# Second block's layer norms: shift and factors read in PSUM, weight folded in, bias on ScalarE, two buffers for squares, another order of halves

## The chip, the cores and the metric

The kernel runs on one core of a Trainium2 chip. Its time is the device time of one execution in microseconds; the number that counts is the median over runs.

## The reference, cut to what matters

512 tokens with 1024 features go through two blocks. The change is in the second, at three of its layer norms: the one after the first feed-forward (ln1), the one of the convolution branch (conv_ln) and the one after the mixer (ln2).

```python
def layer_norm(x, g, b):
    mu = jnp.mean(xf, axis=-1, keepdims=True)
    var = jnp.mean(jnp.square(xf - mu), axis=-1, keepdims=True)
    y = (xf - mu) * lax.rsqrt(var + LN_EPS) * g + b

x = layer_norm(alpha * x + 0.5 * swiglu_ffn(x, ...), ln1_g, ln1_b)
m = hybrid_mixer(x, ...)        # its conv branch: silu(layer_norm(u, conv_ln_g, conv_ln_b)) @ w_conv_o
x = layer_norm(alpha * x + m, ln2_g, ln2_b)
x = layer_norm(alpha * x + 0.5 * swiglu_ffn(x, ...), ln3_g, ln3_b)
```

## The kernel before

Activations lie features on partitions: x[0] to x[7] are eight tiles of 128 features by 512 tokens. A projection takes weight tiles of 1 MB or 768 KB (raw), which ScalarE casts to a high part (whi) and VectorE or GpSimd subtracts to a low part (wlo); the operand X is kept as two parts too (Xh by a cast on ScalarE, L291, Xl by a subtraction, L294). Each 128 x 128 block is then three matmuls, Xh with whi (L354), Xl with whi (L355), Xh with wlo (L356). A projection to 1024 features runs in four chunks c of two output tiles, over kt blocks k. The order on each engine is made by the program's scheduler from the order of the code and the dependences; the pictures of it stand in the section on the change.

**Ln** is the layer norm. Sums over features are sums over partitions, so TensorE makes them: tok_sum multiplies an accumulator by a column (1 column of output for every 128 tokens, L202), which puts tokens on partitions. To bring a factor back, diag_of (L189) makes a diagonal matrix of it on VectorE, and spread (L196, L197) multiplies by ones and copies the result from PSUM to SBUF on ScalarE. The steps: pre adds two tiles to st_a; shift1 and shift2 make a rough mean of these (self.s); center subtracts it from each x (L254), squares it on ScalarE into st_q (L261), adds that to st_b on GpSimd (VectorE for the last two, L263) and adds x to st_a on VectorE (L264); fin1 makes mean, variance and the reciprocal root (rstd_of, L172 to L181, with a square root on ScalarE at L174) and two diagonals; fin2 spreads both; norm multiplies (L287) and subtracts (L288). rstd_of also serves the root-mean-square norms and the heads.

**halved** runs the projection ahead of ln1 (kt=6, operand A) and of ln2 (kt=8), in two halves of 256 tokens, HV0 and HV1: for half 0 chunks 0, 1, 2, 3, for half 1 chunks 3, 0, 1, 2. After each chunk the residual is added (L1383). Half 0's centers follow its chunks 2 and 3; its fin1, fin2 and norms lie among half 1's chunks. apply(k) is norm, then weight and bias (VectorE L1433 for even k, ScalarE L1431 for odd k), then the split into Xh and Xl (Xl on GpSimd). **begin** starts the next projection: 48 matmuls of half 0, fin1 of half 1, 24 matmuls, fin2, 24 matmuls, apply of half 1 for all k, then half 1's matmuls. The conv branch's norm cl is an Ln over all 512 tokens: its centers lie in ret_out's chunks, fin1 to norm in the gate stage that follows.

Of the kernel before, what the change touches and what calls it, by code (L numbers as in the profile page):

```python
# [10 lines left out]
F32 = mybir.dt.float32  # L11
# [3 lines left out]
AF = mybir.ActivationFunctionType  # L15
# [34 lines left out]
def tile_net(ctx: ExitStack, tc: tile.TileContext, a, out):  # L50
# [16 lines left out]
    def bank(shape=(P, T), dt=F32):  # L67
        return ps.tile(list(shape), dt, tag="ps", name=nm("ps"))
# [98 lines left out]
        c = prm[name] + i  # L167
        return par[:, c:c + 1]

    def rstd_of(ss, n, eps, scale=1.0):  # L170
        v = sm.tile([P, n], F32, tag="rs_v", name=nm("rv"))
        vec.tensor_scalar(v, ss, scale, eps, op0=ALU.mult, op1=ALU.add)  # L172
        s = sm.tile([P, n], F32, tag="rs_s", name=nm("rs"))
        act.activation(s, v, AF.Sqrt)  # L174
# [24 lines left out]
    def tok_sum(acc, w, tr=FULL):  # L199
        st = bank((P, tr[1] - tr[0]))  # L200
        for i in range(*tr):
            pe.matmul(st[:, i - tr[0]:i - tr[0] + 1], acc[:, i * P:(i + 1) * P], w, start=True, stop=True)  # L202
        return st

    def stile(tag):
        return xp.tile([P, T], F32, tag=tag, name=nm(tag))

    class Rms:
# [21 lines left out]

    class Ln:
        def __init__(self):
            self.sum, self.sq, self.s, self.rb = [stile(f"st_{c}") for c in "absr"]
            self.started = set()
            self.dg, self.dg2 = {}, {}

        def cols(self, tr):
            return slice(tr[0] * P, tr[1] * P)
# [5 lines left out]
        def shift1(self, tr=FULL):  # L244
            st = tok_sum(self.sum, inv_q, tr)
            self.dg[tr] = diag_of(st, tr)

        def shift2(self, tr=FULL):
            spread(self.dg[tr], self.s, tr)

        def center(self, m, tr=FULL, last=False):
            c = self.cols(tr)
            xm = x[m][:, c]
            vec.tensor_tensor(xm, xm, self.s[:, c], op=ALU.subtract)  # L254
            if tr not in self.started:
                self.started.add(tr)
                act.activation(self.sq[:, c], xm, AF.Square)
                act.copy(self.sum[:, c], xm)
            else:
                q = stile("st_q")  # L260
                act.activation(q[:, c], xm, AF.Square)  # L261
                eng = vec if last else pool
                eng.tensor_tensor(self.sq[:, c], self.sq[:, c], q[:, c], op=ALU.add)  # L263
                vec.tensor_tensor(self.sum[:, c], self.sum[:, c], xm, op=ALU.add)  # L264

        def fin1(self, tr=FULL):
            n = tr[1] - tr[0]
            sd = tok_sum(self.sum, inv_d, tr)
            sv = tok_sum(self.sq, inv_d, tr)
            d = sm.tile([P, n], F32, tag="ln_d", name=nm("lnd"))  # L270
            vec.tensor_copy(d, sd)
            v = sm.tile([P, n], F32, tag="ln_v", name=nm("lnv"))
            vec.tensor_tensor(v, d, d, op=ALU.mult)
            vec.tensor_tensor(v, sv, v, op=ALU.subtract)
            r = rstd_of(v, n, LN_EPS)
            self.dg[tr] = diag_of(r, tr)
            vec.tensor_tensor(d, d, r, op=ALU.mult)
            self.dg2[tr] = diag_of(d, tr)

        def fin2(self, tr=FULL):  # L280
            spread(self.dg[tr], self.rb, tr)
            spread(self.dg2[tr], self.s, tr)

        def norm(self, m, tr=FULL):
            c = self.cols(tr)
            xm = x[m][:, c]
            vec.tensor_tensor(xm, xm, self.rb[:, c], op=ALU.mult)  # L287
            vec.tensor_tensor(xm, xm, self.s[:, c], op=ALU.subtract)  # L288
# [1055 lines left out]
    ple(1, X, rms, lambda m: split(XB.h[m], XB.l[m], x[m], lo=pool))  # L1344


    def swiglu_up(fp, X, t0, nt, first=None):
        A = act_tiles(fp, "A", nt)
        for c in range(nt // 2):
            accs = first if c == 0 else None  # L1350
            if accs is None:
                accs = []
                for _ in range(2):
                    w = W()
                    ac = [bank() for _ in range(2)]
# [11 lines left out]
    def halved(X, kt, ln, apply):  # L1367
        ws = [None] * 4
        for h, tr in enumerate(HV):
            hs = slice(256 * h, 256 * h + 256)  # L1370
            Xh = Act([t[:, hs] for t in X.h], [t[:, hs] for t in X.l])
            order = ((0, 1, 2, 3), (3, 0, 1, 2))[h]
            ms = [2 * c + j for c in order for j in range(2)]
            for t, c in enumerate(order):
                accs = [bank((P, 256)) for _ in range(2)]
                if h == 0:
                    ws[c] = W(kt, hold=c == 3)
                mm_fm(accs, ws[c], Xh, list(range(kt)))
# [24 lines left out]
    def begin(X, ln, apply):  # L1403
        ws, accs = [W(), W(hold=True)], []
# [420 lines left out]
```

## Time and profile before

| | us |
|---|---|
| runs before, median (lowest to highest) | 2817.63 (2815.61 to 2818.87) |
| profiled execution, its time | 2815.37 |
| profiled execution, span from first to last instruction | 2813.6 |
| TensorE busy in the span | 2709.8 |
| VectorE, ScalarE, GpSimd busy | 1608.2, 987.6, 671.5 |
| mean granted clock of TensorE | 0.981 |

A share of busy time is a mean over many stages; which engine sets the end in a stage is read from what TensorE waits for in it, and from how many matmuls it gets through in a window.

### The profile page before, as it was taken

What the parts mean: (1) busy time and instruction counts of PE and PEld (TensorE: products, weight loads), DVE (VectorE), ACT (ScalarE), POOL (GpSimd) and SP (SyncE); (2) the same over time, 40 slices, a digit from 0 to 9 for tenths busy, and PEclk for the clock granted to TensorE, in tenths of its full rate; (3) what the DMA queues carried; (4) which work ended last, traced back from release to release, by engine and by line L of the source; (5) the groups of instructions that cost most, each with busy time, mean ns of one, the idle gap of its engine ahead of it and who ended that gap; (6) DMA issues with size and microseconds to landing.
All of it is one profiled execution on the core that took longest, in us unless ns stands there. A gap on an engine that the chain in (4) does not pass through costs nothing.

```text
span 2813.6 us, 35122 instructions
## 1 busy us (share of the span) xinstructions
PE 2709.8 (96%) x14363; PEld 2293.3 (82%) x14363; DVE 1608.2 (57%) x2526; ACT 987.6 (35%) x1287; POOL 671.5 (24%) x590
## 2 busy tenths in 40 slices
PE   8999999999579999999999998999999899999998
PEld 8978888878468888888888887887888778889898
DVE  6456868676664746475333346965478664733335
ACT  5544424345223423244212234333343352431222
POOL 2213045761441000011000035344444321300000
PEclk9999999999789999999999999999999999999999
DMA  5203333433753232223232222232222223222222
GB/s 161 76 31 106 105 111 133 173 118 126 251 173 100 90 100 95 90 95 130 90 105 90 93 87 73 87 100 77 96 81 82 75 90 114 74 98 90 90 92 74
DMA packets 277842, 289.83 MB, mean 103 GB/s; under 512 B 20197, under 2 KB 266951, under 8 KB 277680
## 3 DMA queue, kind: packets, MB, share of 16 engines
q1 hardware_dynamic: 256208, 260.38, 28.9%
q10 hardware_dynamic: 20640, 26.78, 2.7%
q8 instruction: 113, 1.85, 0.3%
q0 software_dynamic: 832, 0.41, 0.1%
q14 instruction: 49, 0.40, 0.0%
HBM read 263.43 MB, written 24.12 MB: 102 GB/s over the span
## 4 chain that ended last, share of the span: by engine, by line
PE 86%; DVE 6%; POOL 2%; issue 2%; DMA 2%; ACT 2%; SPq 0%; POOLq 0%; DVEq 0%; ACTq 0%
PE ps L354 23%; PE ps L355 23%; PE ps L356 23%; PE ps L363 4%; PE ps L365 4%; PE ps L364 4%; DVE ps L1491 1%; PE ps L635 1%; PE ps L1552 1%; PE ps L659 1%; DVE x L287 1%; POOL st_b L263 1%; PE ps L1116 1%; DMA hd<-h 0%; ACT whi L328 0%
## 5 line engine op out<-in xcount | busy, mean ns | idle before, releaser
L328 ACT CAST whi<-raw 128x2048 fp32r<-128x2048 f32 (+2 forms) x216 | 406.2, 1881 | 763.4 <-PE ps L355 608.4
L354 PE MATMUL ps<-Xh,whi 128*128 128x512 f32 (+1 forms) x1472 | 571.3, 389 | 6.8 <-ACT Xh L291 5.1
L356 PE MATMUL ps<-Xh,wlo 128*128 128x512 f32 (+1 forms) x1472 | 566.3, 385 | 3.1 <-DVE wlo L331 3.1
L355 PE MATMUL ps<-Xl,whi 128*128 128x512 f32 (+1 forms) x1472 | 566.7, 385 | 2.7 <-POOL Xl L294 2.7
L331 DVE TENSOR_TENSOR wlo<-raw,whi 128x2048 fp32r<-128x2048 f32 (+2 forms) x167 | 381.0, 2281 | 324.1 <-ACT whi L328 320.2
L331 POOL TENSOR_TENSOR wlo<-raw,whi 128x2048 fp32r<-128x2048 f32 (+1 forms) x49 | 223.5, 4561 | 689.6 <-ACT whi L328 377.7
L354 PEld LDWEIGHTS ps<-Xh,whi 128*128 128x128 f32 x1472 | 278.7, 190 | 65.4 <-ACT Xh L291 5.5
L356 PEld LDWEIGHTS ps<-Xh,wlo 128*128 128x128 f32 x1472 | 279.2, 190 | 60.7 <-DVE wlo L331 4.4
L355 PEld LDWEIGHTS ps<-Xl,whi 128*128 128x128 f32 x1472 | 279.3, 190 | 59.5 <-POOL Xl L294 3.6
L355 PE MATMUL ps<-XBl,whi 128*128 128x512 f32 (+1 forms) x736 | 283.3, 385 | 2.6 <-POOL XBl L294 2.6
L354 PE MATMUL ps<-XBh,whi 128*128 128x512 f32 (+1 forms) x736 | 282.6, 385 | 1.4 <-ACT XBh L291 1.4
L356 PE MATMUL ps<-XBh,wlo 128*128 128x512 f32 (+1 forms) x736 | 282.5, 385 | 0.0
L355 PE MATMUL ps<-Al,whi 128*128 128x512 f32 (+1 forms) x528 | 203.7, 386 | 3.2 <-DVE Al L294 3.2
L354 PE MATMUL ps<-Ah,whi 128*128 128x512 f32 (+1 forms) x528 | 203.6, 388 | 1.2 <-ACT Ah L291 1.2
L356 PE MATMUL ps<-Ah,wlo 128*128 128x512 f32 (+1 forms) x528 | 203.5, 386 | 0.0
L1491 DVE SCALAR_TENSOR_TENSOR ps<-glu,par,ps 128x512 f32<-128x512 f32 x232 | 174.3, 751 | 4.2
L355 PEld LDWEIGHTS ps<-XBl,whi 128*128 128x128 f32 x736 | 139.8, 190 | 31.6 <-POOL XBl L294 3.4
L354 PEld LDWEIGHTS ps<-XBh,whi 128*128 128x128 f32 x736 | 139.4, 190 | 29.3 <-ACT XBh L291 1.8
L356 PEld LDWEIGHTS ps<-XBh,wlo 128*128 128x128 f32 x736 | 139.8, 190 | 28.0
L220 POOL TENSOR_TENSOR st_a<-st_a,st_q 128x512 f32<-128x512 f32 x25 | 44.3, 1770 | 487.9 <-ACT st_q L218 487.8
L363 PE MATMUL ps<-whi,Xh 128*128 128x256 f32 (+1 forms) x512 | 147.7, 289 | 0.7 <-ACT z L597 0.4
L364 PE MATMUL ps<-wlo,Xh 128*128 128x256 f32 (+1 forms) x512 | 145.0, 284 | 0.0
(472 smaller groups left out, 4869.7 us busy)
## 6 DMA issues: line engine op xcount, KB each, us to landing
raw<-in_ffn_w_up_dram SPq DMA_DIRECT2D x66, 1024.0 KB, 5.1
raw<-in_w_in_dram SPq DMA_DIRECT2D x40, 1024.0 KB, 5.2
raw<-in_ffn_w_down_dram SPq DMA_DIRECT2D x32, 1024.0 KB, 4.9
raw<-in_ffn_w_gate_dram SPq DMA_DIRECT2D x22, 1024.0 KB, 5.2
tab<-tabs ACTq DMA_DIRECT2D x16, 960.0 KB, 4.1
raw<-in_ffn_w_down_dram SPq DMA_DIRECT2D x16, 768.0 KB, 4.2
raw<-in_ev_w_in_dram SPq DMA_DIRECT2D x8, 1024.0 KB, 5.2
raw<-in_ple_w_gate_dram SPq DMA_DIRECT2D x8, 1024.0 KB, 4.9
```

The lines of the kernel that those rows point to most:

```text
L220: eng.tensor_tensor(self.acc, self.acc, sq, op=ALU.add)
L263: eng.tensor_tensor(self.sq[:, c], self.sq[:, c], q[:, c], op=ALU.add)
L287: vec.tensor_tensor(xm, xm, self.rb[:, c], op=ALU.mult)
L328: cp = act.copy(hi, rv)
L331: lo.tensor_tensor(lw, rv, hi.bitcast(F32), op=ALU.subtract)
L354: pe.matmul(acc, wh[j][:, s], X.h[k], start=start and t == 0, stop=False)
L355: pe.matmul(acc, wh[j][:, s], X.l[k], start=False, stop=False)
L356: pe.matmul(acc, wl[j][:, s], X.h[k], start=False, stop=stop and t == len(ks) - 1)
L363: pe.matmul(acc, X.h[k][:, s], wh[j], start=start and t == 0, stop=False)
L364: pe.matmul(acc, X.h[k][:, s], wl[j], start=False, stop=False)
L365: pe.matmul(acc, X.l[k][:, s], wh[j], start=False, stop=stop and t == len(ks) - 1)
L1491: vec.scalar_tensor_tensor(x[m] if t == 30 else acc, u[:, t:t + T], col("ck", t * KD + m), acc, op0=ALU.mult, op1=ALU.add)
```

## The change

- rstd_of takes five VectorE operations instead of six, and may be given tiles for v and t; Rms and Ln give it PSUM ones.
- wide spreads a diagonal into a PSUM bank, and nobody copies it: the centers read the shift there, the norms the factors. Both factors of a half lie in one tile f, one diagonal of 512 columns, one matmul.
- norm is two SCALAR_TENSOR_TENSOR operations with a PSUM operand and with the weight g folded in; the bias is added on ScalarE for every k.
- Squares go to st_q and st_s by turns.
- In halved, half 0's chunks 0 and 1 both run over k up to kt-3 first, and over the last two k afterwards; the first chunk's weights are asked for earlier in the code (early). In half 1 the norms of half 0 stand ahead of the centers of half 1.

```diff
-    def rstd_of(ss, n, eps, scale=1.0):
+    def rstd_of(ss, n, eps, scale=1.0, v=None, t=None):
...
-        vec.reciprocal(r, s)
-        t = sm.tile([P, n], F32, tag="rs_t", name=nm("rt"))
-        vec.tensor_tensor(t, r, r, op=ALU.mult)
-        vec.tensor_tensor(t, t, v, op=ALU.mult)
-        vec.tensor_scalar(t, t, -0.5, 1.5, op0=ALU.mult, op1=ALU.add)
-        vec.tensor_tensor(r, r, t, op=ALU.mult)
+        vec.reciprocal(r, t)
+        vec.scalar_tensor_tensor(t, v, -0.5, r, op0=ALU.mult, op1=ALU.mult)
+        vec.tensor_tensor(t, t, r, op=ALU.mult)
+        vec.scalar_tensor_tensor(r, t, 1.5, r, op0=ALU.add, op1=ALU.mult)
...
+        def wide(self, dg):
+            b = bank((P, dg.shape[1] * P))
+            pe.matmul(b, ones, dg.rearrange("p i t -> p (i t)"), start=True, stop=True)
+            return b
+
         def shift2(self, tr=FULL):
-            spread(self.dg[tr], self.s, tr)
+            self.sh = self.wide(self.dg[tr])
...
-            vec.tensor_tensor(xm, xm, self.s[:, c], op=ALU.subtract)
...
+            vec.tensor_tensor(xm, xm, self.sh, op=ALU.subtract)
...
-                q = stile("st_q")
+                q = stile(("st_q", "st_s")[n % 2])
...
+            st = bank((P, 3, n))
+            sd, sv, t = [st[:, i] for i in range(3)]
+            tok_sum(self.sum, inv_d, tr, sd)
+            tok_sum(self.sq, inv_d, tr, sv)
             d = sm.tile([P, n], F32, tag="ln_d", name=nm("lnd"))
             vec.tensor_copy(d, sd)
...
+            vec.tensor_tensor(t, sd, d, op=ALU.mult)
+            vec.tensor_copy(d, t)
+            vec.scalar_tensor_tensor(sv, sv, LN_EPS, d, op0=ALU.add, op1=ALU.subtract)
+            r = rstd_of(None, n, LN_EPS, v=sv, t=t)
+            f = sm.tile([P, 2 * n], F32, tag="ln_f", name=nm("lnf"))
+            act.copy(f[:, 0:n], r)
+            vec.scalar_tensor_tensor(f[:, n:], sd, -1.0, r, op0=ALU.mult, op1=ALU.mult)
+            self.dg[tr] = [diag_of(f[:, i:i + NT]) for i in range(0, 2 * n, NT)]
...
+        def norm(self, m, tr=FULL, g=1.0):
+            xm = x[m][:, self.cols(tr)]
+            vec.scalar_tensor_tensor(xm, xm, g, self.rb, op0=ALU.mult, op1=ALU.mult)
+            vec.scalar_tensor_tensor(xm, self.s, g, xm, op0=ALU.mult, op1=ALU.add)
...
+                if h == 0 and t < 2:
+                    n = kt - 2
+                    if t == 0:
+                        ws[1] = W(kt)
+                        pair[1] = [bank((P, 256)) for _ in range(2)]
+                        for z in range(2):
+                            mm_fm(pair[z], ws[z], Xh, list(range(n)), stop=False)
+                    mm_fm(accs, ws[c], Xh, [n, n + 1], start=False, js=[n, n + 1])
+                else:
+                    mm_fm(accs, ws[c], Xh, list(range(kt)))
...
                     ln.shift2(tr)
-                    for m in ms[:6]:
-                        ln.center(m, tr)
-                else:
-                    for m in ms[6:]:
-                        ln.center(m, tr, last=True)
                 if h == 1 and t > 0:
                     for k in range(3 * t - 3, min(3 * t, KD)):
                         apply(k, HV[0])
+                if t == 2:
+                    for m in ms[:6]:
+                        ln.center(m, tr)
+                elif t == 3:
+                    for m in ms[6:]:
+                        ln.center(m, tr, last=True)
...
-            ln.norm(k, tr)
-            if k % 2:
-                act.activation(x[k][:, c], x[k][:, c], AF.Identity, scale=col(g, k), bias=col(b, k))
-            else:
-                vec.tensor_scalar(x[k][:, c], x[k][:, c], col(g, k), col(b, k), op0=ALU.mult, op1=ALU.add)
+            ln.norm(k, tr, col(g, k))
+            act.activation(x[k][:, c], x[k][:, c], AF.Identity, bias=col(b, k))
```

TensorE at the start of ln1's halved, before: the last blocks of chunk 0 (the buffers Ah_11918 to Ah_11920 are k = 3 to 5).

```order
L354 MATMUL ps_12310<-Ah_11918,whi_12229 128x256
L355 MATMUL ps_12310<-Al_11924,whi_12229 128x256
L356 MATMUL ps_12310<-Ah_11918,wlo_12230 128x256
L354 MATMUL ps_12309<-Ah_11919,whi_12229 128x256
L355 MATMUL ps_12309<-Al_11925,whi_12229 128x256
```

The same place after (Ah_11884 is k = 3, Ah_11881 is k = 0; whi_12195 is chunk 0's weight, wr_12251 and wr_12252 are chunk 1's).

```order
L365 MATMUL ps_12290<-Ah_11884,whi_12195 128x256
L366 MATMUL ps_12290<-Al_11890,whi_12195 128x256
L367 MATMUL ps_12290<-Ah_11884,wlo_12196 128x256
L365 MATMUL ps_12305<-Ah_11881,wr_12251 128x256
L366 MATMUL ps_12305<-Al_11887,wr_12251 128x256
```

Where k = 4 of chunk 0 followed, k = 0 of chunk 1 follows now; 24 matmuls of chunk 1 stand ahead of the first that takes k = 4.

VectorE in half 1 of ln1, before (x_72 to x_79 are x[0] to x[7]; L287, L288 and L1433 are half 0's norm and weight, L254 half 1's centers).

```order
L287 TENSOR_TENSOR x_76<-x_76,st_r_10439 128x256
L287 TENSOR_TENSOR x_77<-x_77,st_r_10439 128x256
L1383 TENSOR_TENSOR x_74<-x_74,ps_12690 128x256
L1383 TENSOR_TENSOR x_75<-x_75,ps_12691 128x256
L288 TENSOR_TENSOR x_76<-x_76,st_s_10438 128x256
L254 TENSOR_TENSOR x_78<-x_78,st_s_10438 128x256
L254 TENSOR_TENSOR x_79<-x_79,st_s_10438 128x256
L254 TENSOR_TENSOR x_72<-x_72,st_s_10438 128x256
L254 TENSOR_TENSOR x_73<-x_73,st_s_10438 128x256
L264 TENSOR_TENSOR st_a_10436<-st_a_10436,x_79 128x256
```

The same place after (L298 and L299 are the norm, ps_12628 holds the factors, ps_12685 the shift).

```order
L1408 TENSOR_TENSOR x_74<-x_74,ps_12645 128x256
L1408 TENSOR_TENSOR x_75<-x_75,ps_12646 128x256
L298 SCALAR_TENSOR_TENSOR x_76<-x_76,par,ps_12628 128x256
L262 TENSOR_TENSOR x_78<-x_78,ps_12685 128x256
L299 SCALAR_TENSOR_TENSOR x_76<-ps_12628,par,x_76 128x256
L298 SCALAR_TENSOR_TENSOR x_77<-x_77,par,ps_12628 128x256
L262 TENSOR_TENSOR x_79<-x_79,ps_12685 128x256
L299 SCALAR_TENSOR_TENSOR x_77<-ps_12628,par,x_77 128x256
L272 TENSOR_TENSOR st_a_10404<-st_a_10404,x_79 128x256
L262 TENSOR_TENSOR x_72<-x_72,ps_12685 128x256
```

The norms of x[4] and x[5], of which the second came after six centers, stand among the first two centers now, and all others of half 1 come behind; x[6] and x[7] follow the last two residual adds.

ScalarE at fin1 of half 0 in ln1, before (L174 is the square root).

```order
L261 ACTIVATE st_q_12546<-x_79 128x256 [waits DVE_49]
L328 CAST whi_12590<-raw_12425 128x2048 [waits DMAHW0_49,PE_49]
L174 ACT_TABLE_LOAD
L174 ACTIVATE rs_12610<-rv_12608 128x2 [waits DVE_49]
L328 CAST whi_12878<-raw_12588 128x2048 [waits DMAHW1_49,PE_49]
```

The same place after (ps_12562 is the bank with v and t).

```order
L269 ACTIVATE st_s_12511<-x_79 128x256 [waits DVE_49,Pool_49]
L339 CAST whi_12555<-raw_12391 128x2048 [waits DMAHW0_49,PE_49]
L177 ACT_TABLE_LOAD [waits DVE_49]
L177 ACTIVATE ps_12562<-ps_12562 128x2 [waits PE_49]
L287 COPY lnf_12578<-rr_12573 128x2 [waits DVE_49]
```

VectorE's semaphore, which the square root waited for, is now waited for ahead of the table load.

## Rows read from the trace of the kernel before

**Rows 1.** The page: busy time of each engine, and the chain that ended last.

```profile
PE 2709.8 (96%) x14363; PEld 2293.3 (82%) x14363; DVE 1608.2 (57%) x2526; ACT 987.6 (35%) x1287; POOL 671.5 (24%) x590
...
PE 86%; DVE 6%; POOL 2%; issue 2%; DMA 2%; ACT 2%; SPq 0%; POOLq 0%; DVEq 0%; ACTq 0%
```

**Rows 2.** TensorE's waits, 1640 to 1730: us in total, times, longest.

```profile
PE ps L354 <- ACT Xh L291: 5.1, 2, 4.4
PE ps L355 <- DVE Al L294: 3.2, 1, 3.2
PE ps L355 <- POOL Xl L294: 2.7, 3, 1.1
PE ps L202 <- DVE st_a L264: 1.3, 1, 1.3
...
PE ps L196 <- DVE diag L189: 1.1, 1, 1.1
```

**Rows 3.** Windows of 5 us around ln1: busy (instructions) by engine, PEclk, DMA share, GB/s.

```profile
1645.00:1650.00 5.00, 2.86 (x22) 2.46 (x21) 1.78 (x2) 2.51 (x3) 4.03 (x3) 1.00 0.50 157
1650.00:1655.00 5.00, 2.81 (x13) 2.81 (x14) 3.21 (x4) 0.00 (x0) 1.59 (x1) 0.57 0.80 256
1655.00:1660.00 5.00, 5.00 (x34) 5.00 (x34) 0.79 (x2) 0.00 (x0) 0.00 (x0) 0.75 0.20 68
1660.00:1665.00 5.00, 5.00 (x44) 5.00 (x43) 1.26 (x4) 0.00 (x0) 0.00 (x0) 1.00 0.01 3
...
1695.00:1700.00 5.00, 2.25 (x19) 2.05 (x18) 5.00 (x13) 1.87 (x5) 2.07 (x4) 1.00 0.30 79
1700.00:1705.00 5.00, 2.23 (x8) 1.74 (x9) 5.00 (x10) 2.44 (x6) 4.23 (x7) 0.69 0.42 108
1705.00:1710.00 5.00, 5.00 (x23) 4.94 (x24) 4.23 (x15) 1.94 (x5) 1.80 (x2) 0.50 0.00 0
```

**Rows 4.** Timeline, DVE, then POOL: start, us, engine, line, operation, idle before it.

```profile
1677.42 4.52 DVE L172 TENSOR_SCALAR rv<-lnv 128x2 f32<-128x2 f32 x1
...
1677.35 4.57 POOL L331 TENSOR_TENSOR wlo<-raw,whi 128x2048 fp32r<-128x2048 f32 x1 [3.23 <-ACT whi L328]
```

**Rows 5.** Durations by source line: ns min/median/max, first and last start, forms.

```profile
L1383 DVE TENSOR_TENSOR x<-x,ps x32: 406/416/423, 1654.3 to 2425.5; 128x256 f32<-128x256 f32 x32
...
L287 DVE TENSOR_TENSOR x<-x,st_r x40: 409/420/4287, 1685.0 to 2442.8; 128x256 f32<-128x256 f32 x32, 128x512 f32<-128x512 f32 x8
...
L1431 ACT ACTIVATE x<-x,par x16: 585/601/602, 1690.4 to 2444.0; 128x256 f32<-128x256 f32 x16
...
L174 ACT ACT_TABLE_LOAD  x21: 1283/1283/1283, 26.4 to 2773.0; - x21
```

**Rows 6.** Timeline rows of DVE and POOL in ln1; what line 261's squares waited for.

```profile
1666.06 1.43 DVE L254 TENSOR_TENSOR x<-x,st_s 128x256 f32<-128x256 f32 x4 [0.41 <-ACT st_s L197]
...
1717.53 3.73 POOL L294 TENSOR_TENSOR Xl<-x,Xh 128x256 fp32r<-128x256 f32 x4 [8.29 <-ACT Xh L291]
...
  POOL st_b L263: 28.1, 25
```

**Rows 7.** Conv norm: timeline rows of DVE and ACT, then two windows.

```profile
2207.71 6.54 DVE L254 TENSOR_TENSOR x<-x,st_s 128x512 f32<-128x512 f32 x4 [1.54 <-ACT st_s L197]
...
2225.25 0.63 ACT L261 ACTIVATE st_q<-x 128x512 f32<-128x512 f32 x1 [1.67 <-POOL st_b L263]
...
2228.21 3.68 ACT L328 CAST whi<-raw 128x2048 fp32r<-128x2048 f32 x2
...
2225.00:2230.00 5.00, 3.40 (x16) 2.47 (x14) 2.65 (x4) 2.96 (x4) 3.17 (x3) 1.00 0.00 0
2230.00:2235.00 5.00, 3.21 (x8) 2.30 (x9) 4.82 (x4) 3.18 (x3) 0.00 (x0) 0.60 0.25 79
```

**Rows 8.** Two windows in ln2.

```profile
2420.00:2425.00 5.00, 3.49 (x28) 3.09 (x26) 5.00 (x10) 2.36 (x6) 3.53 (x5) 1.00 0.21 77
2425.00:2430.00 5.00, 4.97 (x29) 4.97 (x30) 5.00 (x14) 2.00 (x5) 1.63 (x2) 0.66 0.00 0
```

More of the change, by code (lines that the diff above doesn't have):

```diff
@@ L168, in col @@
         return par[:, c:c + 1]
-    def rstd_of(ss, n, eps, scale=1.0):
[L171 to L174, printed above, removed]
-        r = sm.tile([P, n], F32, tag="rs_r", name=nm("rr"))
-        vec.reciprocal(r, s)
-        t = sm.tile([P, n], F32, tag="rs_t", name=nm("rt"))
-        vec.tensor_tensor(t, r, r, op=ALU.mult)
-        vec.tensor_tensor(t, t, v, op=ALU.mult)
-        vec.tensor_scalar(t, t, -0.5, 1.5, op0=ALU.mult, op1=ALU.add)
-        vec.tensor_tensor(r, r, t, op=ALU.mult)
+    def rstd_of(ss, n, eps, scale=1.0, v=None, t=None):
+        if v is None:
+            v = sm.tile([P, n], F32, tag="rs_v", name=nm("rv"))
+        if ss is not None:
+            vec.tensor_scalar(v, ss, scale, eps, op0=ALU.mult, op1=ALU.add)
+        if t is None:
+            t = sm.tile([P, n], F32, tag="rs_t", name=nm("rt"))
+        act.activation(t, v, AF.Sqrt)
+        r = sm.tile([P, n], F32, tag="rs_r", name=nm("rr"))
+        vec.reciprocal(r, t)
+        vec.scalar_tensor_tensor(t, v, -0.5, r, op0=ALU.mult, op1=ALU.mult)
+        vec.tensor_tensor(t, t, r, op=ALU.mult)
+        vec.scalar_tensor_tensor(r, t, 1.5, r, op0=ALU.add, op1=ALU.mult)
         return r
@@ L197, in spread, with tok_sum @@
         act.copy(o[:, tr[0] * P:tr[1] * P], b)
-    def tok_sum(acc, w, tr=FULL):
-        st = bank((P, tr[1] - tr[0]))
+    def tok_sum(acc, w, tr=FULL, st=None):
+        if st is None:
+            st = bank((P, tr[1] - tr[0]))
         for i in range(*tr):
@@ L223, in fin1 @@
         def fin1(self):
-            self.dg = diag_of(rstd_of(tok_sum(self.acc, inv_d), NT, EPS))
+            st = bank((P, 2, NT))
+            tok_sum(self.acc, inv_d, st=st[:, 0])
+            self.dg = diag_of(rstd_of(st[:, 0], NT, EPS, v=st[:, 0], t=st[:, 1]))
         def fin2(self):
@@ L232, in __init__ @@
         def __init__(self):
-            self.sum, self.sq, self.s, self.rb = [stile(f"st_{c}") for c in "absr"]
-            self.started = set()
-            self.dg, self.dg2 = {}, {}
+            self.sum, self.sq = stile("st_a"), stile("st_b")
+            self.n, self.dg = {}, {}
         def cols(self, tr):
@@ L253, in center @@
             xm = x[m][:, c]
-            vec.tensor_tensor(xm, xm, self.s[:, c], op=ALU.subtract)
-            if tr not in self.started:
-                self.started.add(tr)
+            vec.tensor_tensor(xm, xm, self.sh, op=ALU.subtract)
+            n = self.n[tr] = self.n.get(tr, -1) + 1
+            if n == 0:
                 act.activation(self.sq[:, c], xm, AF.Square)
@@ L267, in fin1 @@
             n = tr[1] - tr[0]
-            sd = tok_sum(self.sum, inv_d, tr)
-            sv = tok_sum(self.sq, inv_d, tr)
+            st = bank((P, 3, n))
+            sd, sv, t = [st[:, i] for i in range(3)]
+            tok_sum(self.sum, inv_d, tr, sd)
+            tok_sum(self.sq, inv_d, tr, sv)
             d = sm.tile([P, n], F32, tag="ln_d", name=nm("lnd"))
             vec.tensor_copy(d, sd)
[L272 to L278, printed above, removed]
-        def fin2(self, tr=FULL):
[L281 to L288, printed above, removed]
+            vec.tensor_tensor(t, sd, d, op=ALU.mult)
[6 more added lines that the diff above has]
+            self.dg[tr] = [diag_of(f[:, i:i + NT]) for i in range(0, 2 * n, NT)]
+        def fin2(self, tr=FULL):
+            n = (tr[1] - tr[0]) * P
+            bs = [self.wide(dg) for dg in self.dg[tr]]
+            self.rb, self.s = bs if n == T else (bs[0][:, 0:n], bs[0][:, n:])
+        def norm(self, m, tr=FULL, g=1.0):
+            xm = x[m][:, self.cols(tr)]
+            vec.scalar_tensor_tensor(xm, xm, g, self.rb, op0=ALU.mult, op1=ALU.mult)
+            vec.scalar_tensor_tensor(xm, self.s, g, xm, op0=ALU.mult, op1=ALU.add)
     def split(dst_h, dst_l, src, lo=None, pin=False):
@@ L1344, in tile_net, with swiglu_up @@
     ple(1, X, rms, lambda m: split(XB.h[m], XB.l[m], x[m], lo=pool))
-    def swiglu_up(fp, X, t0, nt, first=None):
+    def swiglu_up(fp, X, t0, nt, first=None, early=None):
         A = act_tiles(fp, "A", nt)
@@ L1357, in swiglu_up @@
                     accs.append(ac)
+            if early and c == nt // 2 - 1:
+                early()
             for j in range(2):
@@ L1365, in tile_net, with halved @@
     HV = ((0, 2), (2, 4))
-    def halved(X, kt, ln, apply):
-        ws = [None] * 4
+    def halved(X, kt, ln, apply, ws=None):
+        ws = ws or [None] * 4
         for h, tr in enumerate(HV):
@@ L1373, in halved @@
             ms = [2 * c + j for c in order for j in range(2)]
+            pair = {}
             for t, c in enumerate(order):
-                accs = [bank((P, 256)) for _ in range(2)]
-                if h == 0:
+                if c not in pair:
+                    pair[c] = [bank((P, 256)) for _ in range(2)]
+                accs = pair[c]
+                if ws[c] is None:
                     ws[c] = W(kt, hold=c == 3)
-                mm_fm(accs, ws[c], Xh, list(range(kt)))
+                if h == 0 and t < 2:
[8 more added lines that the diff above has]
+                    mm_fm(accs, ws[c], Xh, list(range(kt)))
                 if h == 1 and t == 0:
@@ L1439, in tile_net, with early @@
         for t0, nt in PARTS:
-            A = swiglu_up(fp, XB, t0, nt)
+            down = [None] * 4
+            def early():
+                down[0] = W(nt)
+            A = swiglu_up(fp, XB, t0, nt, early=early if t0 + nt == KF else None)
             if t0 + nt < KF:
@@ L1454, in tile_net @@
                 apply1 = applier(ln, X, "ln1_g_2", "ln1_b_2")
-                halved(A, nt, ln, apply1)
+                halved(A, nt, ln, apply1, down)
     xb.close()
```

## The prediction

> **What bounds the kernel now.** I read the page first: TensorE is busy 2709.8 us of a span of 2813.6, 96%, and 86% of the chain that ended last is its work [rows 1]. So only two things can give time: stretches where TensorE stands still (about 104 us in all), and stretches where the throttle halves its clock. Then the list of waits and the table of windows, for the three layer norms that the change touches. In the first (1645 to 1728 us) TensorE waits 5.1 us for Xh, 3.2 for Al, 2.7 for Xl, 1.3 for st_a and 1.1 for diag [rows 2]. In the windows [rows 3] see two things beside each other: after a window with PE busy only 2.2 to 2.9 of 5 us, the granted clock of the next is 0.50 to 0.75. At full clock a window holds 44 matmuls of 256 columns (0.114 us each), at 0.50 it holds 23. The conv branch's norm has the same pair at 2225 to 2235, the second halved norm at 2420 to 2430 [rows 7, 8]. DVE, ACT and POOL are busy 57, 35 and 24%, so their work costs only where TensorE stands behind it.
>
> Why do they come late there? The timeline shows one cause several times: a DVE operation with all its tensors in SBUF lies still while a POOL tensor operation runs. The two-column rv took 4.52 us, from 1677.42, while POOL's wlo ran 1677.35 to 1681.92 [rows 4]; four shifts at 2207.71 took 6.54 us [rows 7]. Operations with one operand in PSUM never did: 32 residual adds took 406 to 423 ns, while the multiplies by st_r span 409 to 4287 [rows 5]. The second cause: with one buffer st_q, ACT's square waits for POOL's add, 28.1 us in 25 waits [rows 6].
>
> **The change, part by part.** All against the profiled run, 2815.4 us (span 2813.6).
>
> (A) In the first half of ln1, 24 matmuls (chunk 1, k 0 to 3) move ahead of those that wait for Ah and Al. TensorE idles 2.14 + 2.19 us there [rows 3], and the chain that makes Al is not changed, so 24 x 0.114 = 2.7 us fall into the idle time: sure gain 2.7. The idle time left is 1.6 us, and the low clock behind it cost 2.4: 13 matmuls in 2.81 busy us where 13 x 0.114 = 1.5 would do (1.3), and 34 in 5 us (1.1). Does it stay? That bounds A at 2.7 and 5.1; I take 4.0. In ln2 the same move covers nothing, as TensorE doesn't wait there.
>
> (B) Shift read in PSUM, squares in two buffers. The eight centers lose their copy from PSUM, are not blocked, and the squares' chain runs at POOL's pace instead of ACT and POOL by turns. In ln1 that takes the wait for st_a, 1.3 us [rows 2]. Range 0 to 3 (some clock behind it), taken 1.3.
>
> (C) The factors' chain. It keeps its small dependent steps (a copy and a multiply more, some others fewer), all unblocked now as v and t lie in PSUM: of rv's 4.52 us [rows 4] some 4.3 go, and the 1.1 us wait for diag [rows 2] would become 3.2 us of slack. Against that stands a new cost that the order shows: the square root now waits for two engines, so DVE's semaphore stands ahead of the table load, which used to run early. A load takes 1283 ns in all 21 cases [rows 5]: up to 1.28 us in each of three chains. In ln1 that leaves 1.9 us of slack; but diag itself, SBUF only and now 512 columns wide, can be blocked by POOL's wlo (4.57 us) as rv was, and then waits as long as before or longer. I take no change, range -2 to +1.1. In the conv norm and in ln2 TensorE has over 7 us of matmuls between the sums and the factors; there the load is hidden. The Trainium skill (ScalarE: Activation LUTs, What ACT_TABLE_LOAD costs) gives about 2.7 us a load; by that figure C in ln1 would have 0.5 us of slack in place of 1.9, and if diag is blocked besides, the load's other 1.4 us come on top: 2801 where I say 2800. The trace's 1.283 us decides.
>
> (D) The main part: in the second half the norms of the first half stand ahead of the centers, on DVE and so for ACT and POOL. Between 1695 and 1705 TensorE idles 2.75 + 2.77 us, for Xh (4.4 in one wait) and Xl [rows 2, 3]; behind it, 8 matmuls in 2.23 us where 0.9 would do (1.3), and 23 in 5 where 2.6 would do (2.4). Together 9.2 us. After: DVE starts the norms with TensorE still having 72 matmuls (8.2 us) of chunks ahead of begin, and x0 to x5 are done in that time (two operations each; four back to back took 1.43 us [rows 6], where one alone takes 0.41 by its row, so 0.34 each). x6 and x7 stand behind the last residual adds, so their Xl is due some 4.4 to 5.6 us after the last chunk (six to eight DVE operations, 2.0 to 2.7, the bias 0.6, a cast, POOL's 0.93 and what is queued there), where TensorE wants k=6 after 36 matmuls, 4.1: a wait of 0.3 to 1.5. What is queued behind the norms: the centers, and behind these the sums for fin1. From the first norm to the last sum stand 37 DVE operations, 37 x 0.34 = 12.6, and seven sums that are SBUF only, each behind a POOL add of which I count 0.5 (an estimate, half of POOL's 0.93 [rows 6]): some 16. TensorE's cover is 120 matmuls, 13.7. So a wait of about 2 us moves to the sums, and about 1 to diag. Of 9.2 I count 5.5 as gained; range 1 to 9.
>
> (E) Second half's norms in begin(). Now ACT adds all eight biases (0.60 us, of which 0.5 before the next starts; before, DVE scaled the even ones), DVE is not blocked, and POOL's Xl sets the pace: 3.73 us for four, 0.93 each [rows 6]. The first is there about 2.4 us after the factors (two DVE operations, bias, cast, subtraction), the eighth 6.5 later, 8.9. TensorE wants a k each 0.69 us, from 2.7 us on, the eighth at 7.5: a wait of about 1.4, where the rest of Xh and Xl makes 0.7 + 1.6 = 2.3 [rows 2]. Gain 0.9; range -1.4 to 1.5.
>
> (F) Conv norm. Four shifts took 6.54 us behind wlo, then the squares ran at 0.63 + 1.67 = 2.3 us each, and the cast of whi came behind the last of them, at 2228.21 [rows 7]. After, squares follow POOL's adds, and the cast comes some 6 us earlier, so the 1.60 + 1.79 us of idle time go and with them the clock (8 matmuls of 512 columns in 3.21 busy us, at 3.40/16 = 0.2125 each 1.7, so 1.5): 4.9. The order also has two more table loads on ACT, 2 x 1.28, near 2290, which may push a cast of whi: taken 0.9 for them, range 0 to 2.6. Gain 4.0.
>
> (G) ln2. Idle 1.51, then 29 matmuls in 4.97 us where 3.3 would do (1.7) [rows 8]: 3.2 that D's order should remove, with the same new waits behind it. Of its waits in begin I expect little. Taken 2.0, range -2 to 5.
>
> The reciprocal root of the other places is one small operation shorter and lies behind other work: nothing.
>
> Sum: 4.0 + 1.3 + 0 + 5.5 + 0.9 + 4.0 + 2.0 = 17.7; 2815.4 - 17.7 = 2797.7. The median of the three runs is 2817.6, 2.3 above the profiled one; so **2800**.
>
> **Rivals.** First, the waits that D removes come back at the sums. The DVE queue above (16 against 13.7 us) speaks for it, the unblocked PSUM operands against it. Then D gives 2, B, E and G nothing: 4 + 2 + 4 = 10, 2808.
>
> Second, slower: in both halved norms the sums come so late that the whole pair (5.5 us idle and 3.7 of low clock, 9.2) stands there again, 18.4 together, and removes only 9.2 + 3.2 = 12.4: net 6.0. In such a state ACT and POOL are late in begin too (E at -1.4 twice, 2.8), C at -2 and the load exposed once more, 1.3; A gives 2.7 and F 0 as the casts queue behind biases. 2817.6 + 6.0 + 2.8 + 2 + 1.3 - 2.7 = 2827. It decides where the DVE queue from the first norm to the last sum takes over 19 us (13.7 plus the old idle time) instead of 16. Against it: all but the sums and two adds have an operand in PSUM.
>
> Third, the change doesn't do what it says: the shorter chains only let TensorE meet the next late transfer or cast sooner. What is moved ahead is then waited for later: 2816.
>
> **Chances.** Forecast 0.60 (2789 to 2804), waits come back 0.20 (2804 to 2812), no effect 0.12, slower 0.08. The low end has A, D, F and G at their upper bounds (5.1 + 1.3 + 9 + 0.9 + 4.9 + 5 = 26, so 2791) and a little of B and C; the high end takes in the first rival and some of the third. Range 2789 to 2814. A difference of 0.2%, 5.6 us, is about what a measurement can tell from none: faster by more (under 2812) 0.80, within 0.12, slower 0.08.
>
> **What would show it.** In the profile after: no wait for Al over 2 us (A); the first centers in the conv norm under 0.8 us apiece, and no wait for whi near 2225 (F); no wait for Xh over 1.5 us in ln1 (D), and a clock near 1.00 where it was 0.50; a table load directly ahead of its square root, after DVE's step (C). I am wrong if TensorE waits for st_a or diag for over 3 us in begin (first rival, or second where it is over 5), or if the total wait falls as said while whi or wlo waits rise by as much (third).

## The result, and the profile after

| | before | changed kernel |
|---|---|---|
| median (lowest to highest), us | 2818.25 (2815.61 to 2822.27) | 2785.91 (2783.03 to 2786.97) |
| profiled span, us | 2813.6 | 2785.2 |
| ratio of times, 95% interval | | 0.9882 (0.9867 to 0.9896) |

The kernel before has four runs here, one more than in the table ahead of the prediction. The change saves 32 us, where 17.7 were forecast: the direction was right, and the time lies 3 us below the range's low end of 2789. In the profile, TensorE's busy time fell by 12 us, from 2709.8 to 2698.1, and its idle time by 17; both belong to the answer, since a halved clock shows as busy time. The page's line of busy times after, which answers to [rows 1]:

```profile
PE 2698.1 (97%) x14355; PEld 2275.0 (82%) x14355; DVE 1581.5 (57%) x2478; ACT 992.5 (36%) x1295; POOL 666.9 (24%) x590
```

TensorE's waits in ln1 after (1640 to 1730; us in total, times, longest), against [rows 2]:

```profile
PE ps L253 <- DVE diag L190: 1.6, 1, 1.6
PE ps L366 <- DVE Al L305: 1.5, 1, 1.5
PE ps L204 <- DVE st_a L272: 0.6, 1, 0.6
PE ps L366 <- POOL Xl L305: 0.6, 2, 0.3
PE ps L365 <- ACT Xh L302: 0.4, 1, 0.4
```

14.6 us of waits (with 1.2 for Ah, which [rows 2] leaves out) have become 4.7. The same stages in windows of 5 us (busy of PE, PEld, DVE, ACT, POOL, granted clock, DMA share, GB/s), against [rows 3]:

```profile
1655.00:1660.00 5.00, 3.46 (x29) 3.26 (x29) 4.15 (x2) 0.69 (x2) 3.21 (x1) 1.00 0.75 244
1660.00:1665.00 5.00, 5.00 (x45) 5.00 (x44) 2.32 (x6) 0.00 (x0) 0.00 (x0) 1.00 0.52 179
...
1680.00:1685.00 5.00, 3.38 (x25) 2.82 (x24) 3.77 (x8) 2.12 (x2) 4.46 (x2) 1.00 0.39 119
1685.00:1690.00 5.00, 5.00 (x43) 4.95 (x42) 4.68 (x13) 4.10 (x11) 4.93 (x5) 1.00 0.59 192
...
1695.00:1700.00 5.00, 3.73 (x27) 3.09 (x26) 4.53 (x11) 2.98 (x7) 3.28 (x6) 1.00 0.40 119
1700.00:1705.00 5.00, 5.00 (x41) 4.76 (x42) 2.34 (x11) 0.35 (x2) 0.00 (x0) 1.00 0.00 0
```

See the column ahead of the DMA share: the clock is 1.00 in all of them. Before, the clock was at 0.57 and 0.50 around idle times of 4.3 and 5.5 us here [rows 3]; in this profile it does not fall behind idle times of 1.3 to 1.6. That is no rule. A second profile of the same kernel (after2, below) has the same wait of 1.6 us for diag in its window from 1680, and there the clock fell:

```profile
1680.00:1685.00 5.00, 3.38 (x20) 2.47 (x18) 2.88 (x8) 2.09 (x2) 4.46 (x2) 0.85 0.19 51
1685.00:1690.00 5.00, 5.00 (x35) 4.79 (x34) 3.58 (x8) 3.38 (x8) 4.94 (x4) 0.81 0.62 202
```

55 matmuls went through these two windows, and 68 through the same two of the first profile. Nor does a long wait settle it: the first profile has two waits of 3.35 us for rn in the heads, and these are the windows in which they end:

```profile
1915.00:1920.00 5.00, 4.07 (x22) 3.44 (x23) 4.94 (x10) 0.66 (x2) 0.66 (x1) 1.00 0.00 0
...
2170.00:2175.00 5.00, 3.88 (x17) 3.61 (x18) 2.99 (x6) 0.00 (x0) 0.00 (x0) 0.54 0.00 0
```

For places, I take the starts of instructions that both kernels have, and the difference of the time between two of them against before (negative is faster). "ln1" runs from the first product of the first feed-forward to the first convolution tap; "heads" from there to the first sum into part; "conv norm" from there to the last gate; "ln2" from there to the last product of the second feed-forward; "first block" is all ahead of ln1.

| us | first block | ln1 | heads | conv norm | ln2 | span |
|---|---|---|---|---|---|---|
| changed kernel | +4.9 | -17.4 | -3.3 | -7.3 | -4.8 | -28.4 |
| changed kernel, second profile | +5.6 | -14.2 | -1.6 | -7.3 | -5.9 | -24.2 |
| old_order | +3.5 | -18.8 | -1.6 | -7.2 | -8.5 | -33.4 |
| old_order, second profile | +1.9 | -18.8 | -1.7 | -7.1 | -7.5 | -34.0 |
| no_ahead | +4.3 | -10.4 | -2.6 | -7.2 | -6.8 | -23.3 |
| one_square | -0.6 | -13.9 | -3.3 | -6.7 | -3.7 | -29.0 |
| norm_sbuf | +2.3 | -6.2 | -1.8 | -7.1 | -0.3 | -13.6 |
| psum_alone | +1.4 | -9.3 | -1.7 | -6.7 | -8.0 | -25.1 |
| shift_sbuf | +3.4 | -10.8 | -2.1 | -2.0 | +0.5 | -11.8 |
| bias_dve | +3.2 | -10.7 | -2.8 | -7.2 | -3.5 | -21.8 |
| order_only | +0.9 | +0.1 | +0.8 | 0.0 | +4.5 | +6.2 |
| rstd_only | +6.3 | +2.0 | -1.9 | -0.6 | +1.0 | +6.3 |
| best | +2.1 | -21.0 | -3.2 | -7.1 | -6.6 | -36.6 |

The row for the changed kernel sums to its span's 28.4 with -0.5 in the tail. The first block differs by -0.6 to +6.3 between profiles of kernels that hardly differ there, so differences of up to 7 us in it are the spread of single executions, and -17.4 and -14.2 for the same kernel tell how far one ln1 can be trusted: the second profile has the low clock behind its wait for diag, and once more from 1700 to 1710 (0.89 and 0.77). In the heads, -3.3 belongs to the profile in which one of the two long waits kept the clock, and -1.6 to one in which both lost it.

### The profile page after: what moved, and what is told of

Read it like the earlier page. It is cut to its first block, busy times and chain, and to the rows that moved or that the text cites. A ratio compares the mean times of both kernels' runs of the same rounds, so it can differ in the third digit from the quotient of the medians.

```text
span 2785.2 us, 35089 instructions
## 1 busy us (share of the span) xinstructions
PE 2698.1 (97%) x14355; PEld 2275.0 (82%) x14355; DVE 1581.5 (57%) x2478; ACT 992.5 (36%) x1295; POOL 666.9 (24%) x590
```

## Experiments: one part undone at a time

The ratios are against the kernel before, with a 95% interval.

**The order.** The changed kernel with the centers ahead of the norms again (old_order):

```diff
-                if h == 1 and t > 0:
-                    for k in range(3 * t - 3, min(3 * t, KD)):
-                        apply(k, HV[0])
                 if t == 2:
                     for m in ms[:6]:
                         ln.center(m, tr)
                 elif t == 3:
                     for m in ms[6:]:
                         ln.center(m, tr, last=True)
+                if h == 1 and t > 0:
+                    for k in range(3 * t - 3, min(3 * t, KD)):
+                        apply(k, HV[0])
```

> The changed kernel with one part undone: in the second half the centers stand ahead of the first half's norms again. Theory (the order was what took TensorE's waits for Xh and the halved clock behind them): some 9 us come back in ln1 and 3 in ln2, about 2798 us beside 2786; a wait for Xh over 2 us and a granted clock under 0.8 near 1700. Rival (operands in PSUM alone did it, since VectorE is no longer blocked): 2786 to 2788, no such wait.

Measured: 2781.82 us, 0.9868 (0.9853 to 0.9882), and the clock at 1.00 near 1700. Its waits in ln1, whole:

```profile
PE ps L253 <- DVE diag L190: 1.6, 1, 1.6
PE ps L366 <- DVE Al L305: 1.6, 1, 1.6
PE ps L366 <- POOL Xl L305: 0.7, 2, 0.4
```

There is no wait for Xh at all. The prediction's main term is wrong in sign: the new order is not what removed the wait, and the old order with the rest of the change is 4 us faster. Both were then run again on one chip.

> The old order once more, beside the run above on the same chip: 2782. It tells whether it is faster than the changed kernel (2786) by more than the runs spread, and gives the reference for the best version: theory (the new order costs 1 to 4 us in ln1 and ln2) 2781 to 2783; rival (the runs spread by that much) 2784 to 2787.

> The changed kernel once more, on the same chip as the old order: 2786 if the new order costs something, 2782 if the two differ by chance alone. Where the spread of the first block (4 us between profiles) is chance, its step there differs from the first profile's +4.6.

Measured: 2782.0 (2781.43 to 2782.32) and 2787.77 (2785.8 to 2791.78). No run of one lies among the runs of the other. In both profiles of the old order the clock is 1.00 in every window of ln1 and ln2; part of its lead over after2 is that. In ln2, TensorE's waits sum to 2.7 us with the new order (the longest is 1.0 for a cast of whi) and to 0.9 with the old one. The row on the order alone, from the other side, is the kernel before with only this part done:

> The kernel before with one part done: in the second half the first half's norms stand ahead of the centers. Theory (the norms are late because they are blocked, and the order is worth nothing by itself): 2816 to 2821, with a wait for Xh over 3 us in ln1. Rival (the prediction's main term): 5 to 9 us faster, 2809 to 2813, without that wait.

Measured: 2823.7 us, 1.0022 (1.0013 to 1.0032), so slower, by 4.5 us of its profile in ln2. Its wait in ln1 and the windows there:

```profile
PE ps L354 <- ACT Xh L291: 5.8, 2, 5.1
```

```profile
1700.00:1705.00 5.00, 0.05 (x1) 0.05 (x1) 5.00 (x13) 1.94 (x6) 3.17 (x6) 0.86 0.40 97
1705.00:1710.00 5.00, 4.05 (x18) 3.76 (x18) 3.46 (x6) 1.53 (x4) 2.29 (x3) 0.50 0.02 8
```

The norms are ahead of the centers and Xh is late all the same, TensorE idle for almost a whole window with VectorE busy for all of it, and the clock halved behind it.

**The factors in PSUM.** The changed kernel with the two factors copied to SBUF and the norms reading there (norm_sbuf):

```diff
+            if n != T:
+                o = stile("st_r")
+                act.copy(o, bs[0])
+                bs[0] = o
             self.rb, self.s = bs if n == T else (bs[0][:, 0:n], bs[0][:, n:])
```

> The changed kernel with the factors of the two halved norms copied to SBUF by ScalarE, one copy of 512 columns each, and read there. Theory (operations with all tensors in SBUF are blocked while a POOL tensor operation runs): norms up to 1 us each and more behind wlo, 3 to 5 us in all, about 2790. Rival (the order alone suffices, the queue has slack): 2786 to 2787.

Measured: 2804.29 us, 0.9948 (0.9933 to 0.9963): 17 to 18 us of the 32 are given back, four times what theory said. First its longest wait in ln1, then its windows, then a group of its norms by source line (ns min/median/max), and last the same group of the changed kernel:

```profile
PE ps L369 <- ACT Xh L306: 5.3, 3, 4.5
```

```profile
1695.00:1700.00 5.00, 0.67 (x5) 0.47 (x4) 5.00 (x13) 1.89 (x5) 3.08 (x6) 0.89 0.32 105
1700.00:1705.00 5.00, 4.79 (x21) 4.50 (x21) 2.50 (x4) 1.08 (x4) 1.60 (x2) 0.50 0.00 0
1705.00:1710.00 5.00, 5.00 (x28) 5.00 (x28) 2.17 (x10) 0.35 (x2) 0.00 (x0) 0.59 0.00 0
```

```profile
L302 DVE SCALAR_TENSOR_TENSOR x<-x,par,st_r x32: 472/479/3028, 1681.9 to 2431.5; 128x256 f32<-128x256 f32 x32
```

```profile
L298 DVE SCALAR_TENSOR_TENSOR x<-x,par,ps x32: 459/472/483, 1683.7 to 2417.6; 128x256 f32<-128x256 f32 x32
```

The same operation on the same numbers: with a PSUM operand 32 of them lie between 459 and 483 ns; from SBUF the longest takes 3028, and the wait for Xh of the kernel before [rows 2] is back with its halved clock. The longest is the first of this pair on VectorE; it ends 0.3 us after POOL's wlo:

```profile
1681.91 3.42 DVE L302 SCALAR_TENSOR_TENSOR x<-x,par,st_r 128x256 f32<-128x256 f32 x2 [1.51 <-ACT st_r L296]
...
1680.06 4.59 POOL L346 TENSOR_TENSOR wlo<-raw,whi 128x2048 fp32r<-128x2048 f32 x1 [0.54 <-ACT whi L343]
```

The edit also adds ScalarE's copy to the chain, but that takes 0.59 us each time, too little for 17.

**The shift in PSUM.** As above for the centers (shift_sbuf):

```diff
-            self.sh = self.wide(self.dg[tr])
+            self.sh = stile("st_r")[:, self.cols(tr)]
+            act.copy(self.sh, self.wide(self.dg[tr]))
```

> The changed kernel with the shift copied to SBUF by ScalarE and read there by the centers. Theory (in the conv norm the first four centers lie behind POOL's wlo, which makes the squares and the cast of whi late): 5 to 6 us come back in the conv norm, with a wait for whi or wlo there, and 1 to 2 in the halved norms: 2793. Rival (the cast is early for another reason): 2786 to 2787.

Measured: 2801.76 us, 0.9939 (0.9924 to 0.9953), 14 to 16 us slower than the changed kernel and 9 beyond what theory said. Conv norm: 5.3 us come back, with this wait and this row of VectorE's timeline, which answers to the 6.54 us of [rows 7]:

```profile
PE ps L368 <- DVE wlo L343: 3.2, 1, 3.2
```

```profile
2198.45 6.53 DVE L263 TENSOR_TENSOR x<-x,st_r 128x512 f32<-128x512 f32 x4 [1.54 <-ACT st_r L258]
```

That is as theory said for the conv norm. The halved norms are not: 3 to 7 us in ln1 and 5 to 6 in ln2 where 1 to 2 were expected, again with a wait for Xh (3.1 us) and the clock at 0.50 from 1700 to 1705.

**Squares in two buffers.** The changed kernel with st_q alone (one_square; the edit is one line, `q = stile("st_q")`):

> The changed kernel with one buffer for squares. Theory (the squares' chain by turns is what made the cast of whi late in the conv norm): 4 to 5 us come back there and 1 to 2 in ln1, about 2792, with a wait for whi or wlo near the conv norm's centers. Rival (VectorE blocked by POOL was the cause): 2786 to 2787.

Measured: 2789.46 us, 0.9899 (0.9882 to 0.9915), 2 to 4 us slower than the changed kernel by the medians; the runs overlap with those of after2, so by time alone the difference is not shown. The place is not the one expected: the conv norm gives back 0.6 us and shows no wait; in ln1 a wait for Xh of 2.5 us stands there. So, by these profiles, the conv norm's gain is the shift's, not the squares'.

**The bias.** Even k back on VectorE (bias_dve):

```diff
-            act.activation(x[k][:, c], x[k][:, c], AF.Identity, bias=col(b, k))
+            if k % 2:
+                act.activation(x[k][:, c], x[k][:, c], AF.Identity, bias=col(b, k))
+            else:
+                vec.tensor_scalar(x[k][:, c], x[k][:, c], col(b, k), None, op0=ALU.add)
```

> The changed kernel with the bias of even k added on VectorE, from SBUF. Theory: four more operations a half on VectorE, each blocked where POOL runs, 1.4 to 4 us in each queue, of which 1 to 3 in all reach TensorE: 2787 to 2789. Rival (ScalarE and POOL set the pace, so taking work from ScalarE helps): 2783 to 2785.

Measured: 2795.26 us, 0.9916 (0.9902 to 0.9931), 7 to 9 us slower than the changed kernel. The added operations (ns min/median/max), and its windows in ln1:

```profile
L1459 DVE TENSOR_SCALAR x<-x,par x16: 336/733/2214, 1683.5 to 2425.7; 128x256 f32<-128x256 f32 x16
```

```profile
1695.00:1700.00 5.00, 1.26 (x9) 0.85 (x8) 4.96 (x15) 2.81 (x7) 3.62 (x5) 1.00 0.23 54
1700.00:1705.00 5.00, 5.00 (x26) 4.94 (x26) 1.66 (x6) 0.16 (x1) 0.59 (x1) 0.54 0.00 0
```

VectorE takes four operations back in each half, and they last 0.34 to 2.21 us, so the theory's blocking is there and only its price was too low: TensorE waits 3.0 us for Xh and then gets 26 and 31 matmuls into two windows that hold 44 each.

**The matmuls moved ahead.** The changed kernel without them (no_ahead; `if h == 0 and t < 2` becomes `if False`):

> The changed kernel without the matmuls of chunk 1 moved ahead of the wait for Ah and Al. Theory (idle time and the clock behind it, 5.2 us by the two traces): 2791, with an idle time over 3.5 us at the start of ln1 and a clock under 0.8 behind it. Rival (only the 24 matmuls' 2.7 us, the clock stays up): 2788.5.

Measured: 2790.14 us, 0.9896 (0.9882 to 0.9911), 2 to 4 us slower by the medians, with runs that overlap with those of after2; in the profile ln1 is 3.8 to 7.0 us longer than in the two of the changed kernel. The 3.8 is against after2, which has the low clock behind its wait for diag as this profile has (0.80 and 0.86). Its start of ln1:

```profile
1655.00:1660.00 5.00, 1.85 (x9) 1.74 (x9) 3.81 (x2) 0.19 (x1) 2.65 (x1) 0.73 0.79 260
1660.00:1665.00 5.00, 5.00 (x29) 5.00 (x29) 1.26 (x3) 0.00 (x0) 0.00 (x0) 0.59 0.43 151
```

TensorE waits 3.2 us for Al and 1.0 for Ah, and the clock falls to 0.59. That is the theory's case, not the rival's; the time, between the two forecasts, doesn't decide it.

**What is left without three parts.** Old order, nothing moved ahead, one buffer (psum_alone):

> The changed kernel with three parts undone: the old order in the second half, no matmuls moved ahead, one buffer for squares. What is left are the reads in PSUM, the shorter reciprocal root, the weight folded in and the bias on ScalarE. Theory (the reads in PSUM carry the greater part by themselves): 2782 of the old order, 7 more for the matmuls not moved and 4 for the squares: 2793, with no wait for Xh over 3 us in ln1. Rival (they work only with the new order or the second buffer): 2803 or more.

Measured: 2791.69 us, 0.9904 (0.9887 to 0.992). 27 of the 32 us are there with the reads in PSUM, the bias on ScalarE, the folded weight, the shorter root and the earlier request of weights; the longest wait for Xh in ln1 is 1.0 us. The clock is at 0.50 in the window behind it all the same, and at 0.66 behind the wait for Al (3.1 us).

**The reciprocal root alone**, in the kernel before:

> The kernel before with one part done: the reciprocal root with five small operations instead of six. Theory (each step of it stands among larger operations on VectorE, so one step less takes 0.7 us off each of the four waits for rn): 2 to 3 us faster, 2815 to 2816. Rival (the root lies behind other work, as predicted): 2817.6 to 2818.7, and the four waits for rn sum to 11 us or more as before.

Measured: 2818.42 us beside 2819.99, 0.9996 (0.9987 to 1.0005): no difference that can be told. The four waits for rn do fall, first before, then rstd_only:

```profile
PE ps L1592 <- DVE rn L1585: 11.5, 4, 4.1
```

```profile
PE ps L1590 <- DVE rn L1583: 8.4, 4, 3.4
```

0.8 us each, as theory said of the waits; its 2 to 3 us faster did not come. "heads" is 1.6 to 3.3 us shorter in all kernels that have the root; by time alone that isn't confirmed.

**A better version.** From what was found: the old order, the product ahead of Al written to PSUM, and f in PSUM (best):

```diff
-            f = sm.tile([P, 2 * n], F32, tag="ln_f", name=nm("lnf"))
+            f = st[:, 3:5].rearrange("p a n -> p (a n)")
...
-                vec.scalar_tensor_tensor(g, g, 0.5, accs[1][j], op0=ALU.mult, op1=ALU.mult)
+                if early and c == nt // 2 - 1:
+                    vec.scalar_tensor_tensor(accs[1][j], g, 0.5, accs[1][j], op0=ALU.mult, op1=ALU.mult)
+                    g = accs[1][j]
+                else:
+                    vec.scalar_tensor_tensor(g, g, 0.5, accs[1][j], op0=ALU.mult, op1=ALU.mult)
```

> The changed kernel with the old order in the second half, and three more operands moved to PSUM or ahead: the last chunk's product ahead of Al is written to PSUM, the factors' column f lies in PSUM, and a square root of one column after half 0's last squares loads the table early. Theory (what is left in ln1, 1.6 us of Al and 1.6 of diag, are blocked operations too): some 3 us under the old order alone, 2779, with neither wait over 0.5 us. Rival (the casts of Ah and whi are what is late): 2782, the waits as before.

Measured: 2778.48 us, 0.9852 (0.9837 to 0.9866), the fastest of all, 3.5 under the old order. Two rows of VectorE for the same subtraction, of the changed kernel and of best:

```profile
1655.21 4.15 DVE L305 TENSOR_TENSOR Al<-swg,Ah 128x512 fp32r<-128x512 f32 x2 [2.97 <-ACT Ah L302]
```

```profile
1652.52 1.29 DVE L305 TENSOR_TENSOR Al<-ps,Ah 128x512 fp32r<-128x512 f32 x2 [2.99 <-ACT Ah L302]
```

POOL's wlo runs beside both pairs. With one operand in PSUM the pair takes 1.29 us, and the wait for Al is gone. The wait for diag is 0.8 in place of 1.6, not under 0.5. The third part, a square root meant to load the table early, did nothing: the scheduler put it at the program's start (0.7 us), and the load stayed where it was.

## Why the prediction was wrong

The direction held. The cause that its opening names, VectorE's SBUF operations lying behind POOL, is what the runs show as the greater part; the sum then gave it the small terms (B 1.3 and E 0.9) and gave the order the large one. By stages, the forecast has 11.7 us in ln1 (A to E), 4.0 in the conv norm, 2.0 in ln2 and nothing in the heads; the two profiles have 17.4 and 14.2, 7.3 and 7.3, 4.8 and 5.9, 3.3 and 1.6. The signs that it named for itself all came (Al 1.5 us, Xh 0.4, the centers of the conv norm under 0.7), but they could not tell the order from the operands in PSUM: old_order shows them too. Step by step:

- **D**, "the main part: in the second half the norms of the first half stand ahead of the centers", 5.5 us for ln1, failed. The idle time and the clock behind it did go (idle 5.5 to 1.3 us, clock 0.69 and 0.50 to 1.00), but by other parts: undone one at a time, against the two profiles of the changed kernel, the factors in PSUM are worth 8.0 to 11.2 us in ln1, the bias 3.5 to 6.7, the shift 3.4 to 6.6, the squares 0.3 to 3.5. The order alone gave 0 in ln1 and lost in ln2; undone, it made the kernel 4 us faster. What the step overlooked: a queue of norms that is blocked again and again (8 of the 32 multiplies by st_r of 256 columns took 0.95 us or more before) is late in either order.
- The parts undone one at a time add up to more than they are worth together. Each of them but the order brings a wait of 2.5 us or more back in its profile of ln1, with a low clock behind it (0.50 to 0.72 in a window); psum_alone, without A, the order and the second buffer, has 27 of the 32 us. The prediction counted part of the wait and part of the clock for each (5.5 of 9.2, 4.0 of 6.7). The clock's loss does not go in proportion to a wait: behind 1.6 us for diag it was there in one profile and not in another of the same kernel, and behind 3.35 us for rn once and once not in a single profile. What makes the difference, no run here shows.
- **A**: 4.0 taken, bounds 2.7 and 5.1. The idle time went from 4.3 to 1.5 us and the clock stayed up, so the two traces give 5.2, just over the upper bound; undone, 3.8 to 7.0.
- **B**: 1.3 taken, bounds 0 and 3. Half 0's wait for st_a (1.3 us) is gone, and so, in the first profile, is a low clock behind it that B's figure left out: 0.80 and 0.86 from 1675 to 1685 before, some 2 us. The 0.6 of after is half 1's, and new with the order. The parts that B prices gave back 0.3 to 3.5 (squares) and 3.4 to 6.6 (shift) in ln1 when undone, because the norms of the other half stand in the same queue. Mis-sized.
- **C**: the number was right, the reason only in part. The wait for diag went from 1.1 to 1.6, within -2 and +1.1. Rows of ScalarE and VectorE after:

```profile
1675.40 1.90 ACT L339 CAST whi<-raw 128x2048 fp32r<-128x2048 f32 x1 [1.25 <-PE ps L366]
1677.35 1.28 ACT L177 ACT_TABLE_LOAD   x1
...
1678.84 0.17 DVE L179 RECIPROCAL rr<-ps 128x2 f32<-128x2 f32 x1 [1.56 <-ACT ps L177]
...
1681.04 1.49 DVE L190 TENSOR_TENSOR diag<-cst,lnf 128x512 f32<-128x512 f32 x1
```

  The load stands between VectorE's step (1677.11) and the reciprocal, 1.28 us as all others. It is not the semaphore that holds it there: ScalarE was at its cast of whi until 1677.30, when VectorE's step had just ended. diag takes 1.49 us, from 1681.04; POOL's wlo (1677.38 to 1681.97) ends within it, and half 1's diag, with POOL idle, took 0.69.

  The Trainium skill (ScalarE: Activation LUTs, What ACT_TABLE_LOAD costs) gives about 1283 ns for the load itself, and about 2.66 us for a switch of tables with a drain, which is the 2.7 of the prediction. The trace agrees on the load and shows no drain: from the end of the cast (1677.30) to the start of the square root (1678.65) are 1.35 us.
- **E**: 0.9 taken, upper bound 1.5. The waits in begin's second half went from 2.3 us to 0.3, so 2.0, where a wait of 1.4 was forecast to stay. The pace of Xl was as forecast, one every 0.91 us (0.74 on POOL and 0.17 of waiting for ScalarE's cast); TensorE's demand was not. It stayed busy from its first Xl to the eighth, 0.9 us a k and not 0.69.
- **F**: 4.0 taken, 4.9 at most; 7.3 measured. The idle time and the clock behind it are gone, and the two table loads cost nothing visible. The sum had left out a wait of 0.7 us for wlo near 2290 and a third window at a low clock, 1.2 us by the same working (18 matmuls of 0.2125 us in 5.00):

```profile
2235.00:2240.00 5.00, 5.00 (x18) 3.97 (x17) 0.87 (x1) 0.00 (x0) 0.00 (x0) 0.72 1.00 325
```

  The mechanism was half right: the shift does it, and the squares 0.6 us at most.
- **G**: 2.0 taken, 4.8 and 5.9 measured, and 7.5 to 8.5 with the old order: the same mistake as D, and a term put at nothing. "Of its waits in begin I expect little" passed over 2.3 us of idle time in the second half before, with a low clock behind it; after, 0.3 us is left and the clock stays at 1.00.

```profile
2440.00:2445.00 5.00, 3.50 (x24) 2.89 (x23) 4.66 (x10) 2.15 (x6) 3.38 (x4) 1.00 0.00 0
2445.00:2450.00 5.00, 5.00 (x30) 4.90 (x29) 0.00 (x0) 3.09 (x5) 1.64 (x3) 0.66 0.00 0
```

- "Nothing" for the reciprocal root: the waits for rn fell by 3.1 us in sum. Its steps stand among larger operations on VectorE, so one less took 0.8 us and not 0.2.

Neither the first nor the second rival came: the wait for st_a was 0.6 and not 3 or 5. The third did not either.

What stays open: of the 3 us that the order costs in ln2, the waits explain some 2 (2.7 against 0.9); why the cast of whi comes late there is not worked out. The earlier request of weights, the folded weight and the single diagonal were never undone by themselves. No experiment took POOL's wlo away from VectorE's SBUF operations, so that the blocking is POOL's doing rests on the rows' coincidence in time and on the PSUM operand curing it.

## What to carry to other kernels

Where two engines share SBUF, look for the same operation at very different durations (409 to 4287 ns here) before looking at its order: giving it an operand in PSUM was worth far more than moving it. Price a wait together with the clock behind it, and give the clock a range from nothing to all: one wait of 1.6 us had the low clock behind it in one execution and not in another. Any one of several parts left out may bring a long wait back. Look for signs that tell your main term from its neighbours, and undo the parts one by one even when the whole is faster; here one of six was a loss.

## What the runs showed of the hardware

A VectorE operation with an operand in PSUM kept its duration (459 to 483 ns in 32 norms, 406 to 422 in 32 residual adds of the changed kernel), and the same norms with all in SBUF did not (472 to 3028), the longest while POOL's wlo ran. POOL's subtraction of 128 x 256 took 0.73 to 0.74 us in begin after, where four took 3.73 before; that the two hold each other up both ways is argued from this, not tested. The granted clock did not follow the length of a wait: behind 1.6 us for diag it stayed at 1.00 in one profile of the changed kernel and fell to 0.85 and 0.81 in the other, and behind two waits of 3.35 us it stayed at 1.00 once and fell to 0.54 once. Its lower level is 0.50; a value between is the mean of a window that has both.
